# Gated expert values rounded by VectorE alone, one weight split behind them, and the next expert's row gathers put earlier

## The chip, the cores and the metric

The kernel runs on one core of one Trainium2 chip. The metric is device time: the median of three runs of the kernel before is 3069.16 us (3065.15 to 3070.6). The profile below is of one further execution of 3062.2 us.

## The reference, cut to what matters

The program is one transformer block: a projection, a chunked retention and a dilated attention, their merge, a layer norm, and then a mixture of 16 experts (4 groups of 4; each token takes 2 experts of one group), again with a layer norm behind it. All data are float32, sequence 2048, width 1024, expert width 512. The change touches only the experts:

```python
def expert_block(args):
    xblk, e = args
    hid = jax.nn.silu(xblk @ w_gate[e]) * (xblk @ w_up[e])
    return hid @ w_down[e]
```

Each token's result is weighted, added into the token's row, and the last layer norm follows.

## The kernel before

A float32 product is made of three passes of TensorE on rounded operands (type fp32r): each operand x is held as a rounded part hi and a rest lo = x - hi, and the passes are hi by hi, hi by lo, lo by hi (`passes`). Making such a pair is called a split. `split` (lines 86 to 89) lets ScalarE (ACT) write hi by a copy (line 88) and VectorE (DVE) write lo by a subtraction (line 89). In the listings a split of a weight piece is one 128x1024 row at L88 and one at L89.

The experts run one after the other, 0 to 15, in `MoE.run`; in this part of the program all engines keep the order in which the code is written. For one expert the program does this:

- `gate_up`, four times (quarters m = 0 to 3): 48 matmuls of 128x256 each (line 1288) put the gate and the up values of 256 tokens into one bank of PSUM.
- `hidden(m)`, written one quarter later than its products: ACT takes the silu of the gate half out of PSUM into a buffer s (line 1294), DVE multiplies s by the up half (line 1295), and s is split into hi and lo (lines 88 and 89).
- `part`: 36 matmuls of 128x512 (line 1315) multiply quarters 0, 1 and 2 of the hidden values by the down weights into four banks; 12 more follow for quarter 3.
- `weights(n)`: takes the next n weight pieces of 512 KB, which SP's queue has loaded into one of four raw buffers, splits each, and lets SP load the piece that is four further on into the buffer so freed (lines 1207 and 1208). An expert has 12 pieces. In quarters 0 and 1 they are the four down pieces of this expert, in quarters 2 and 3 the first two gate/up pieces of the next expert. Four more are taken in `two`, two more behind it.
- `fetch(e + 1)`: two gathers of 128 rows (line 1226, issued by POOL) bring the next expert's token rows. `turn(e + 1)` later transposes them on TensorE (line 1263) and splits them on ACT and DVE.
- `next(fin)`: one step of the last layer norm of tokens of the group of four experts before (statistics L859 and L867, two POOL operations L868 and L869, two DVE operations L1417 and L1419, and a scatter by POOL to the output, L1231). There is such work in experts 4 to 7, 8 to 11 and 12 to 15, a step in each of the first three quarters and one at the end of an expert.
- Experts with more than 256 tokens take `three` in place of `two` (in this data 3, 7, 8, 10, 11); there a branch (L1513) comes between `part` and the transposes.

POOL's DMAs (gathers, and scatters that add into `d_z`) run on the software queue q0, SP's on the hardware queue q1; both are served by the same 16 DMA engines.

Of the kernel before, what the change touches and what calls it, by code (L numbers as in the profile page):

```python
# [40 lines left out]
class Ring:  # L41
# [4 lines left out]
    def next(self):  # L46
        v = self.views[self.i % len(self.views)]
        self.i += 1
        return v
# [36 lines left out]
def split(nc, hi, lo, src, sub=None):  # L86

    nc.scalar.activation(hi, src, AF.Copy)  # L88
    (sub or nc.vector).tensor_sub(lo, src, hi)  # L89
# [1080 lines left out]
class MoE:  # L1170
# [120 lines left out]

    def hidden(self, m, ps):
        nc, s = self.g.nc, self.sr.next()
        nc.scalar.activation(s, ps[:, :256], AF.Silu)
        nc.vector.tensor_mul(s, s, ps[:, 256:])
        split(nc, *(t[:, m, :] for t in self.h), s)

    def down(self, h, idx, tag="main", sums=None, then=None, wait=True):

# [8 lines left out]
    def banks(self, blocks, tag="main"):  # L1308
        return [(b, j, self.g.bank(tag)) for b in blocks for j in range(2)]
# [170 lines left out]
    def blocks(self, e, wg, idx, fin):  # L1480

        p = []
        for m in range(4):
            p.append(self.gate_up(wg[m]))
            if m == (3 if e < NE - 1 else 2):
                self.hint(e)
            if m:
                self.hidden(m - 1, p[m - 1])
            self.weights((2, 2, 1, 1)[m])
            if m < (3 if e < NE - 1 else 1):  # L1490
                next(fin, None)
            if m == 2:
                self.fetch(e + 1)
                for b in range(2) if e % 4 == 3 else ():
                    self.gather(self.sums[b], self.g.d_z, idx[:, b, 0:1])
                if e % 4 == 3 and e < NE - 1:
                    self.list(e // 4)
                if e == NE - 2:
                    self.list(3)
        return p[3]  # L1500
# [269 lines left out]
```

## Time and profile before

| what | value |
|---|---|
| median of 3 runs | 3069.16 us |
| the profiled execution | 3062.2 us, span 3060.0 us |
| TensorE (PE) busy | 2915.3 us, 95% of the span |
| DVE, ACT, POOL busy | 1429.4, 974.4, 663.8 us |
| mean granted TensorE clock | 0.978 |
| stretch of experts 1 to 14 | 2332 to 3005 us |

A row of the timeline gives the start in us, the duration in us, the engine, the line, the operation, what it writes and reads, how many instructions are merged in it, and in brackets how long the engine sat idle before it and what ended that. A row of the waits gives the waiting engine and line, what it waited for, the sum in us, the times, and the longest. Names: `moe` are buffers of the experts (hidden values, token rows), `mw` and `m2w` are weights (raw and split), `d_x` holds the token rows, `d_z` the sums.

### The profile page before, as it was taken

The page shows a single profiled execution, that of the slowest core. Times are in us where ns is not written, and L with a number is a line of the kernel's source. Part 1 is how long each engine was busy: PE and PEld are TensorE (multiplying, and loading weights), DVE is VectorE, ACT ScalarE, POOL GpSimd, SP SyncE. Part 2 cuts the span into 40 slices and gives each one's busy share as a digit, 9 for nine tenths or more (in the row PEclk, how much of TensorE's full clock was granted, in tenths as well). Part 3 has the DMA queues.
Part 4 walks back from the last instruction along what each step waited for, and adds up shares of the span by engine and source line. Part 5 has one row for each costly group of instructions (what it writes and reads, how often), then busy time and mean ns, then how long its engine had stood idle before and what let it go on. Part 6 is the DMA issues. An engine that isn't in the chain of part 4 may idle for free. (4 is left out here: it accounts for less than half of the span.)

```text
span 3060.0 us, 44087 instructions
## 1 busy us (share of the span) xinstructions
PE 2915.3 (95%) x16140; PEld 2516.4 (82%) x16140; DVE 1429.4 (47%) x3259; ACT 974.4 (32%) x1945; POOL 663.8 (22%) x720
## 2 busy tenths in 40 slices
PE   8999999999999999999889999989998999989997
PEld 6887888888888888888668888878877988878886
DVE  3222433233335523334545665556554476444565
ACT  3221223233333322332123333323224444333342
POOL 0001311122113322100222112222432223022133
PEclk9999999999999999999899999999998999999998
DMA  6445956855766675545853444355847768365684
GB/s 208 142 181 161 199 144 161 178 142 143 160 161 164 176 162 144 143 117 175 284 204 135 155 152 141 124 176 207 146 131 204 253 216 270 124 192 168 202 275 160
DMA packets 449147, 534.14 MB, mean 175 GB/s; under 512 B 183153, under 2 KB 292849, under 8 KB 446818
## 3 DMA queue, kind: packets, MB, share of 16 engines
q1 hardware_dynamic: 261538, 417.78, 43.3%
q0 software_dynamic: 187328, 112.79, 16.1%
q8 instruction: 155, 2.54, 0.4%
q14 instruction: 126, 1.03, 0.1%
HBM read 378.12 MB, written 151.76 MB: 173 GB/s over the span
## 5 line engine op out<-in xcount | busy, mean ns | idle before, releaser
L144 PE MATMUL bank_main<-h,h 128*128 128x512 f32 x3936 | 1019.0, 403 | 10.6 <-ACT h L88 5.8
L144 PEld LDWEIGHTS bank_main<-h,h 128*128 128x128 f32 x3936 | 716.1, 190 | 149.4 <-DVE h L89 8.2
L361 ACT ACTIVATE at<-at,at 128x256 f32<-128x256 f32 (+2 forms) x384 | 174.4, 455 | 536.5 <-DVE at L359 495.9
L1288 PE MATMUL bank_main<-moe,m2w 128*128 128x256 f32 x2304 | 276.5, 281 | 7.5 <-DVE moe L1323 4.8
L1288 PEld LDWEIGHTS bank_main<-moe,m2w 128*128 128x128 f32 x2304 | 274.6, 188 | 10.2 <-issue 6.0
L359 DVE CUSTOM_DVE_ANT_0 at<-bank_att,at 128x256 f32<-128x256 f32 (+2 forms) x384 | 124.9, 362 | 214.7 <-PE bank_att L352 135.5
L1315 PE MATMUL bank_main<-mw,moe 128*128 128x512 f32 x744 | 195.9, 420 | 24.1 <-ACT moe L88 23.9
L1315 PEld LDWEIGHTS bank_main<-mw,moe 128*128 128x128 f32 x744 | 147.4, 203 | 61.9 <-ACT moe L88 27.8
L1083 PE MATMUL bank_main<-m2w,m 128*128 128x512 f32 x768 | 195.0, 407 | 1.2 <-DVE m L89 1.2
L744 PE MATMUL bank_main<-m1r,m1r 128*128 128x512 f32 x672 | 189.7, 415 | 0.0
L379 PEld LDWEIGHTS bank_att<-at,at 128*128 128x128 f32 (+1 forms) x1280 | 168.9, 192 | 13.3 <-DVE at L371 1.9
L89 DVE TENSOR_TENSOR h<-h,h 128x1024 fp32r<-128x1024 f32 x108 | 134.9, 1254 | 80.3 <-ACT h L88 79.6
L1083 PEld LDWEIGHTS bank_main<-m2w,m 128*128 128x128 f32 x768 | 144.2, 193 | 33.8 <-DVE m L89 1.9
L379 PE MATMUL bank_att<-at,at 128*128 128x64 f32 (+1 forms) x1280 | 164.4, 267 | 1.3 <-DVE at L371 1.3
L352 PE MATMUL bank_att<-at,at 128*128 128x256 f32 (+2 forms) x768 | 152.7, 326 | 3.1 <-DVE at L381 3.1
L381 DVE COPY at<-bank_att 128x128 f32<-128x128 f32 x192 | 55.4, 288 | 212.3 <-PE bank_att L379 208.8
L352 PEld LDWEIGHTS bank_att<-at,at 128*128 128x128 f32 x768 | 142.1, 233 | 13.5 <-DVE at L381 3.9
L320 POOL DMA_DIRECT2D at<-d_q x96 | 77.6, 811 | 339.6 <-PE bank_att L352 333.2
L744 PEld LDWEIGHTS bank_main<-m1r,m1r 128*128 128x128 f32 x672 | 125.2, 188 | 25.1
L319 POOL DMA_DIRECT2D at<-d_k x64 | 51.0, 814 | 417.2 <-PE bank_att L352 207.4
L89 DVE TENSOR_TENSOR m2w<-mw,m2w 128x1024 fp32r<-128x1024 f32 x78 | 95.8, 1237 | 94.0 <-ACT m2w L88 94.0
L88 ACT ACTIVATE h<-h 128x1024 fp32r<-128x1024 f32 x108 | 113.2, 1055 | 79.9 <-PE bank_main L144 45.0
(295 smaller groups left out, 4382.0 us busy)
## 6 DMA issues: line engine op xcount, KB each, us to landing
mw<-in_w_gu_dram SPq DMA_DIRECT2D x98, 512.0 KB, 6.4
h<-in_w_in_dram SPq DMA_DIRECT2D x92, 512.0 KB, 6.1
mw<-in_w_dn_dram SPq DMA_DIRECT2D x49, 512.0 KB, 5.8
at<-d_q POOLq DMA_DIRECT2D x96, 256.0 KB, 12.4
at<-d_k POOLq DMA_DIRECT2D x64, 256.0 KB, 13.8
at<-d_va SPq DMA_DIRECT2D x240, 64.0 KB, 4.2
moe<-in_w_gu_dram SPq DMA_DIRECT2D x30, 512.0 KB, 5.8
d_o<-at SPq DMA_DIRECT2D x192, 66.0 KB, 4.0
```

Of the source, the lines that this page charges most:

```text
L88: nc.scalar.activation(hi, src, AF.Copy)
L89: (sub or nc.vector).tensor_sub(lo, src, hi)
L144: self.g.nc.tensor.matmul(ps, s[:, k, c], m[:, k % 2, :], start=k + n == 0, stop=k * 3 + n == 23)
L320: done.append(nc.gpsimd.dma_start(Q[i][:, c], ap3(g.d_q, order * 1024 * T + o, [[512 * T, 2], [T, 64], [1, 512]])))
L352: nc.tensor.matmul(ps[:, e, :nk], queries(Q[e]), keys(k), start=n == 0, stop=n == 1)
L359: nc.vector.tensor_tensor_reduce(out=pe, in0=ps[:, e, :nk], in1=bv, scale=1.0, scalar=3e38, op0=OP.add, op1=OP.min, accum_out=ot[:, 128 + ...
L361: nc.scalar.activation(pe, pe, AF.Exp, scale=-1.0, bias=ot[:, 128 + e:129 + e], accum_out=ot[:, 130 + e:131 + e])
L379: nc.tensor.matmul(po[:, 64 * e:64 * e + 64], pt[:cw, e, c, :], v[:cw, c, 64 * e:64 * e + 64], start=c == 0, stop=c == nch - 1)
L744: nc.tensor.matmul(ps, a[:, kk:kk + 128], w[:, c], start=k == ks[0] and i == 0, stop=k == ks[-1] and i == 2)
L1083: nc.tensor.matmul(ps[j], a[:, kk], w[:, c], start=k + i == 0, stop=k * 3 + i == 23)
L1288: nc.tensor.matmul(ps[:, 256 * u:256 * u + 256], x[:, k, c], y[:, k, :], start=k + i == 0, stop=k * 3 + i == 23)
L1315: self.g.nc.tensor.matmul(p, a[:, k, 128 * b:128 * b + 128], w[:, 512 * j:512 * j + 512], start=k + i == 0, stop=k * 3 + i == 11)
```

## The change

`hidden` no longer uses `split`: DVE multiplies s by the up half twice, once with a rounded output (hi) and once back into s, and subtracts. In `blocks`, quarter 2 splits no weight piece and quarter 3 splits two. The gathers of the next expert's rows (and in experts 3, 7, 11 and 15 of the sums) are written in quarter 1, ahead of that quarter's layer norm step, and no longer in quarter 2 behind it.

```diff
--- before.py
+++ after.py
@@ -1291,9 +1291,11 @@
 
     def hidden(self, m, ps):
         nc, s = self.g.nc, self.sr.next()
+        hi, lo = (t[:, m, :] for t in self.h)
         nc.scalar.activation(s, ps[:, :256], AF.Silu)
+        nc.vector.tensor_mul(hi, s, ps[:, 256:])
         nc.vector.tensor_mul(s, s, ps[:, 256:])
-        split(nc, *(t[:, m, :] for t in self.h), s)
+        nc.vector.tensor_sub(lo, s, hi)
 
     def down(self, h, idx, tag="main", sums=None, then=None, wait=True):
 
@@ -1482,17 +1484,18 @@
         p = []
         for m in range(4):
             p.append(self.gate_up(wg[m]))
+            if m == 1:
+                self.fetch(e + 1)
+                for b in range(2) if e % 4 == 3 else ():
+                    self.gather(self.sums[b], self.g.d_z, idx[:, b, 0:1])
             if m == (3 if e < NE - 1 else 2):
                 self.hint(e)
             if m:
                 self.hidden(m - 1, p[m - 1])
-            self.weights((2, 2, 1, 1)[m])
+            self.weights((2, 2, 0, 2)[m])
             if m < (3 if e < NE - 1 else 1):
                 next(fin, None)
             if m == 2:
-                self.fetch(e + 1)
-                for b in range(2) if e % 4 == 3 else ():
-                    self.gather(self.sums[b], self.g.d_z, idx[:, b, 0:1])
                 if e % 4 == 3 and e < NE - 1:
                     self.list(e // 4)
                 if e == NE - 2:
```

The order on DVE in expert 10, from the hidden values of quarter 1 to the second gate/up piece (`m2w_14802`). `moe_17011` and `moe_17012` are hi and lo, `moe_17027` and `moe_17028` the two buffers s, `moe_17048` and `moe_17049` two token rows in the layer norm. Before:

```order
L1295 TENSOR_TENSOR moe_17028<-moe_17028,bank_main 128x256
L89 TENSOR_TENSOR moe_17012<-moe_17028,moe_17011 128x256
L89 TENSOR_TENSOR m2w_14802<-mw_14991,m2w_14801 128x1024
L1419 SCALAR_TENSOR_TENSOR moe_17048<-moe_17048,moe_17051,moe_17047 128x1024
L867 BN_AGGR moe_17052<-moe_17052 128x2
L1417 SCALAR_TENSOR_TENSOR moe_17049<-moe_17049,moe_17052,moe_17046 128x1024
L1295 TENSOR_TENSOR moe_17027<-moe_17027,bank_main 128x256
L89 TENSOR_TENSOR moe_17012<-moe_17027,moe_17011 128x256
L89 TENSOR_TENSOR m2w_14802<-mw_14992,m2w_14801 128x1024
```

And now:

```order
L1296 TENSOR_TENSOR moe_17011<-moe_17028,bank_main 128x256
L1297 TENSOR_TENSOR moe_17028<-moe_17028,bank_main 128x256
L1298 TENSOR_TENSOR moe_17012<-moe_17028,moe_17011 128x256
L1421 SCALAR_TENSOR_TENSOR moe_17048<-moe_17048,moe_17051,moe_17047 128x1024
L867 BN_AGGR moe_17052<-moe_17052 128x2
L1419 SCALAR_TENSOR_TENSOR moe_17049<-moe_17049,moe_17052,moe_17046 128x1024
L1296 TENSOR_TENSOR moe_17011<-moe_17027,bank_main 128x256
L1297 TENSOR_TENSOR moe_17027<-moe_17027,bank_main 128x256
L1298 TENSOR_TENSOR moe_17012<-moe_17027,moe_17011 128x256
L89 TENSOR_TENSOR m2w_14802<-mw_14991,m2w_14801 128x1024
L89 TENSOR_TENSOR m2w_14802<-mw_14992,m2w_14801 128x1024
```

The subtraction of the first gate/up piece has gone from in front of L1419 (now L1421) to behind the hidden values of quarter 2, and each multiplication is there twice.

The order on POOL in the same expert, from the scatter of a finished row on; `moe_17013` and `moe_17014` are the two buffers of the next expert's rows. Before:

```order
L1231 DMA out_dram<-moe_17057,moe_17022 2560x1024
L1504 TENSOR_LOAD const_83
L868 TENSOR_SCALAR moe_17051<-moe_17051 128x1
L869 TENSOR_TENSOR moe_17051<-moe_17051,const_80 128x1
L1231 DMA out_dram<-moe_17048,moe_17059 2560x1024
L868 TENSOR_SCALAR moe_17052<-moe_17052 128x1
L869 TENSOR_TENSOR moe_17052<-moe_17052,const_80 128x1
L1226 DMA moe_17013<-d_x_72,moe_17018 128x1024
L1226 DMA moe_17014<-d_x_72,moe_17018 128x1024
```

And now:

```order
L1231 DMA out_dram<-moe_17057,moe_17022 2560x1024
L1507 TENSOR_LOAD const_83
L1226 DMA moe_17013<-d_x_72,moe_17018 128x1024
L1226 DMA moe_17014<-d_x_72,moe_17018 128x1024
L868 TENSOR_SCALAR moe_17051<-moe_17051 128x1
L869 TENSOR_TENSOR moe_17051<-moe_17051,const_80 128x1
L1231 DMA out_dram<-moe_17048,moe_17059 2560x1024
L868 TENSOR_SCALAR moe_17052<-moe_17052 128x1
L869 TENSOR_TENSOR moe_17052<-moe_17052,const_80 128x1
```

The two gathers have moved past two pairs of L868 and L869 and one scatter to the output.

## Rows read from the trace of the kernel before

**Rows 1.** The first line of the page.

```profile
span 3060.0 us, 44087 instructions
```

**Rows 2.** Waits of PE from expert 1 to expert 14 (2332 to 3028 us), three of them.

```profile
PE bank_main L1315 <- ACT moe L88: 19.0, 8, 5.2
PE bank_att L1263 <- DMA moe<-d_x,moe: 7.8, 4, 2.7
PE bank_att L1263 <- PEq L1513: 6.2, 4, 2.5
```

**Rows 3.** Stretches of one expert each, from its first gate/up matmul to the first of the next: experts 2, 4, 5, 6, 9, 13 and 14. Columns: start and end, length, then busy time with instruction count of PE, PE's weight load, DVE, ACT and POOL, the granted clock, the share of the DMA engines' time, GB/s.

```profile
2368.00:2403.40 35.40, 35.40 (x257) 33.41 (x256) 19.79 (x24) 19.48 (x29) 6.52 (x6) 1.00 0.85 274
2460.20:2495.80 35.60, 35.56 (x256) 33.56 (x257) 27.83 (x36) 14.74 (x23) 7.80 (x8) 1.00 0.64 224
2495.80:2538.20 42.40, 38.88 (x258) 35.39 (x257) 27.53 (x34) 19.66 (x29) 16.25 (x14) 0.92 0.81 262
2538.20:2577.80 39.60, 36.16 (x257) 33.19 (x256) 27.34 (x34) 19.44 (x29) 13.51 (x12) 1.00 0.80 254
2714.20:2757.90 43.70, 38.51 (x256) 35.15 (x257) 27.33 (x34) 20.05 (x30) 18.32 (x15) 0.92 0.84 262
2923.50:2964.30 40.80, 37.67 (x258) 34.35 (x257) 27.24 (x34) 19.64 (x29) 15.48 (x14) 0.96 0.83 267
2964.30:3004.90 40.60, 37.28 (x257) 34.54 (x256) 27.53 (x34) 19.59 (x29) 13.50 (x12) 0.96 0.77 253
```

**Rows 4.** PE's timeline at L1315, in experts 4, 5, 9, 10 (two rows), 11 and 13.

```profile
2483.04 8.42 PE L1315 MATMUL bank_main<-mw,moe 128*128 128x512 f32 x36
...
2520.73 7.16 PE L1315 MATMUL bank_main<-mw,moe 128*128 128x512 f32 x30 [0.66 <-ACT moe L88]
...
2744.05 9.54 PE L1315 MATMUL bank_main<-mw,moe 128*128 128x512 f32 x30 [4.66 <-ACT moe L88]
...
2780.65 1.54 PE L1315 MATMUL bank_main<-mw,moe 128*128 128x512 f32 x6
2785.34 8.73 PE L1315 MATMUL bank_main<-mw,moe 128*128 128x512 f32 x30 [3.15 <-ACT moe L88]
...
2852.53 9.88 PE L1315 MATMUL bank_main<-mw,moe 128*128 128x512 f32 x30 [5.22 <-ACT moe L88]
...
2950.81 8.62 PE L1315 MATMUL bank_main<-mw,moe 128*128 128x512 f32 x30 [3.03 <-ACT moe L88]
```

**Rows 5.** Timeline of expert 10 on ACT and DVE, from the copy of its last down piece to the hidden values of quarter 2.

```profile
2773.94 1.06 ACT L88 ACTIVATE mw<-moe 128x1024 fp32r<-128x1024 f32 x1 [2.83 <-DMA moe<-in_w_dn_dram]
...
2775.03 1.23 DVE L89 TENSOR_TENSOR mw<-moe,mw 128x1024 fp32r<-128x1024 f32 x1 [2.67 <-ACT mw L88]
...
2778.81 0.41 DVE L1295 TENSOR_TENSOR moe<-moe,bank_main 128x256 f32<-128x256 f32 x1
2779.25 0.42 ACT L88 ACTIVATE moe<-moe 128x256 fp32r<-128x256 f32 x1 [3.98 <-DVE moe L1295]
...
2780.65 1.22 DVE L89 TENSOR_TENSOR m2w<-mw,m2w 128x1024 fp32r<-128x1024 f32 x1 [0.52 <-ACT m2w L88]
...
2781.79 1.28 DVE L1419 SCALAR_TENSOR_TENSOR moe<-moe,moe,moe 128x1024 f32<-128x1024 f32 x1
...
2783.22 1.28 DVE L1417 SCALAR_TENSOR_TENSOR moe<-moe,moe,moe 128x1024 f32<-128x1024 f32 x1
...
2784.43 0.41 DVE L1295 TENSOR_TENSOR moe<-moe,bank_main 128x256 f32<-128x256 f32 x1
2784.87 0.42 ACT L88 ACTIVATE moe<-moe 128x256 fp32r<-128x256 f32 x1 [3.99 <-DVE moe L1295]
```

**Rows 6.** The same in expert 11: the multiplication of quarter 1, the copy of the first gate/up piece, the silu of quarter 2.

```profile
2845.42 0.41 DVE L1295 TENSOR_TENSOR moe<-moe,bank_main 128x256 f32<-128x256 f32 x1
...
2849.38 1.06 ACT L88 ACTIVATE m2w<-mw 128x1024 fp32r<-128x1024 f32 x1 [3.10 <-DMA mw<-in_w_gu_dram]
2850.34 0.36 ACT L1294 ACTIVATE moe<-bank_main 128x256 f32<-128x256 f32 x1
```

**Rows 7.** POOL's timeline in expert 10: the last scatter ahead of the layer norm step, its first operation, and the two gathers.

```profile
2763.70 1.72 POOL L1231 DMA_INDIRECT out_dram<-moe,moe  x1 [1.14 <-DVE moe L1419]
2776.47 1.32 POOL L868 TENSOR_SCALAR moe<-moe 128x1 f32<-128x1 f32 x1 [11.04 <-DVE moe L867]
...
2786.68 1.75 POOL L1226 DMA_INDIRECT moe<-d_x,moe  x1 [0.19 <-issue]
2788.73 0.95 POOL L1226 DMA_INDIRECT moe<-d_x,moe  x1 [0.30 <-issue]
```

**Rows 8.** DMA in five stretches. Rows of issues: what is loaded, queue, count, KB, us to landing; the three are issued at 2762.3 (expert 10's last down piece), near 2781.9 (expert 10) and at 2835.4 (expert 11). Rows of queues: packets, MB, share of the 16 engines' time; the first two from 2764 to 2772 us, the third from 2772 to 2775 us.

```profile
moe<-in_w_dn_dram SPq DMA_DIRECT2D x1, 512.0 KB, 11.7
...
q0 software_dynamic: 365, 1.33, 62.4%
q1 hardware_dynamic: 531, 0.99, 38.4%
...
q1 hardware_dynamic: 579, 1.15, 99.6%
...
mw<-in_w_gu_dram SPq DMA_DIRECT2D x1, 512.0 KB, 3.8
...
mw<-in_w_gu_dram SPq DMA_DIRECT2D x1, 512.0 KB, 14.0
```

## The prediction

> **What bounds the kernel now.** I read the page first for the span [rows 1], then PE's waits over the experts, then the experts one by one as windows, and last the timeline of the engines where PE waits. PE is busy 95% of the span, so time can only go where PE stands still or runs at a lower clock. From expert 1 to 14 two waits belong to the edited code [rows 2]: the down products (L1315) wait 19.0 us in 8 places for the ACT copy that writes hi of the hidden values, and the transposes of the next rows (L1263) wait 7.8 us in 4 places for the gather. The windows show the whole price [rows 3]: experts 2 and 4 take 35.4 and 35.6 us with PE never idle, while 5, 6, 9, 13 and 14, with the same products, take 42.4, 39.6, 43.7, 40.8 and 40.6. Their sum is 207.1; five times 35.6 is 178.0; so 29.1 us are lost there, more than the waits alone, since after a wait the granted clock is lower (0.92 in 5 and 9) and matmuls last longer. Experts 10 and 11 go through the branch, so I take them from the matmuls: 30 of them last 7.16 us after a short wait, 8.73 after 3.15 us and 9.88 after 5.22 us [rows 4]. That is 3.15 + 1.57 = 4.7 us and 5.22 + 2.72 = 7.9 us. In both, the lost time is 1.5 times the wait; I use that factor below. In all 29.1 + 4.7 + 7.9 = 41.7 us are within reach. The third wait of [rows 2], 6.2 us at the branch, is one of PE's own sequencer, and I leave it as it is.
>
> Why hi is late is seen in expert 10 [rows 5]. The last down piece lands late and ACT copies it at 2773.94; DVE subtracts at 2775.03, runs its layer norm step, and multiplies quarter 1 at 2778.81. Then come ACT's hi, the rest lo, the subtraction of a gate/up piece (from 2780.65), L1419, L1417, the multiplication of quarter 2 at 2784.43, ACT's hi at 2784.87, and PE at 2785.34. So DVE's order is the limit, with a trip to ACT inside it. In expert 11 it is ACT's order [rows 6]: the silu of quarter 2 stands behind the copy of a gate/up piece that waited 3.10 us for its DMA.
>
> **The change part by part.** *Second multiplication for ACT's copy.* DVE gets one more 0.41 us instruction for each quarter, ACT loses one of 0.42. Before, from the start of the multiplication to the end of lo were 0.41, a hand-over, 0.42, a hand-over and a subtraction of about the same length, 1.3 us; now three DVE instructions make about 1.25. So DVE's chain is no longer, and hi exists 0.45 us earlier.
>
> *Weight split moved.* Its subtraction, with the wait in front of it, took DVE from about 2780.1 to 2781.79, 1.7 us, ahead of quarter 2's values; now it is behind them. The new chain in expert 10: 2778.81 + 1.25 = 2780.06; L1419 takes 1.2 from start to start; from there to the next multiplication are 2784.43 - 2782.99 = 1.44; 2780.06 + 1.2 + 1.44 = 2782.7; the rounded product ends at 2783.1. Before, hi ended at 2785.3: 2.2 us earlier. PE stood ready at 2785.34 - 3.15 = 2782.19, so it waits 0.9 us. With the same 2.2 us, expert 13 goes from 3.03 to 0.8 [rows 4], expert 9 from 5.2 to 3.0, and the waits in 5, 6 and 14 go. (The four long ones make 16.1 of the 19.0 us; of the other 2.9 some 0.5 is a stop in 9 just ahead of its long one, 2.4 are left for 5, 6 and 14.) In expert 11 ACT's silu no longer stands behind the DMA wait: quarter 1's chain starts at 2845.42, quarter 2's follows at about 2846.7 and PE needs it at 2852.53 - 5.22 = 2847.3; nothing is left of that wait. What stays is (3.0 + 0.9 + 0.8) x 1.5 = 7 us.
>
> What the moved split may cost: the piece's raw buffer comes free later, behind quarter 2's lo, so SP loads the piece that is the third of `two` later, and ACT's copies of the turned rows are queued behind that piece's copy; PE's next gate/up products wait for those. The cover is the 36 down products of 8.42 us [rows 4]. By the near row, a load issued at that point of an expert lands in 3.8 us [rows 8]: 1.5 + 1.2 + 3.8 and two copies of 1.06 end about 8.6 us after the down products start, while the turned rows can first be copied near 9.1. Cost nothing to a few tenths; I take 1.5 us in all. The far row is 14.0 us to landing (expert 11, where gathers and scatters ran beside it); that end is a rival.
>
> *Gathers moved.* POOL now issues them behind the scatter of 2763.70 and ahead of L868 at 2776.47, where it sat idle 11.04 us, against 2786.68 and 2788.73 [rows 7]: 20 us earlier. They cost POOL 2.7 us of that idle time. The 7.8 us of waits in 5, 6 and 14 go (their clock loss is in the windows). In experts 3, 7 and 11 POOL had nothing in front of the gathers, so they hardly move. The cost is on the DMA engines: the gathers, 1 MB, now queue on q0 behind the scatters while q1 still has weights to bring. From 2764 to 2772 both queues ran and q1 moved 0.99 MB in 8 us (0.12 MB/us); from 2772 it was alone and moved 1.15 MB in 3 us (0.38) [rows 8]. The last down piece, issued at 2762.3 and landing 11.7 us later, is what DVE's chain begins with. Had it still to come wholly at 0.12 rather than 0.38 MB/us, it would land 0.52/0.12 - 0.52/0.38 = 2.9 us later; but its copy starts at 2773.94, only 2 us after q0 ran empty, and the 0.99 MB are nearly all of the two down pieces in flight. Bounds 0 and 2.9; I take a third of a us in the three experts that still wait, 1 x 1.5 = 1.5 us. On the gain side the later pieces find the engines freer; I leave it at nothing, up to 2 us.
>
> The Trainium skill, page "DMA: Bandwidth & Descriptors", section "Queues, rings and completion order", says that each DMA engine takes turns between the queue rows for which it has work, a packet at a time. The two rates agree with that; by it alone, gathers put beside weight loads always halve them, and the sum would be the first rival's. The trace has both: q0 was nearly drained when the piece landed.
>
> **Sum.** 41.7 - 7 - 1.5 - 1.5 = 31.7 us. The profiled execution of 3062.2 us becomes 3030.5; it stood 7.0 below the median, and I carry the difference over to the median: 3069.2 - 31.7 = 3037.5, said as 3037.
>
> **The rivals.** *Gathers slow the last down piece (chance 0.15).* At 2.9 us the chain is later than the 2.2 us won: 9, 10 and 13 keep their waits of 5.2 + 3.15 + 3.03 = 11.4 us and a little more, about 12 x 1.5 = 18 us instead of 7, and 5, 6, 14 keep 2.4 x 1.5 = 3.6. The gather waits and expert 11 are still won: 41.7 - 18 - 3.6 - 1.5 = 18.6, so 3050.6. For it speaks q1's rate beside q0; against it the order of arrival above.
>
> *The DMA engines bound the experts (0.08).* Their share is 0.81 to 0.84 of 42.4 to 43.7 us [rows 3], that is 34 to 37 us of work for a 35.6 us expert. If 0.86, just over the 0.85 of expert 2, is the most that can be had, 5, 6, 9, 13 and 14 stop at 39.9, 36.8, 42.7, 39.4 and 36.4: 17.2 us remain of the 29.1, the gain is 41.7 - 17.2 - 1.4 = 23, and the time 3046. Against it: the share stood near 1 (62.4 + 38.4%) for 8 us on end, so 0.86 is no ceiling.
>
> *The late pieces in `two` (0.12, of which 0.05 slower).* One mechanism: the two gate/up pieces that are loaded after quarter 2's values land so late that ACT copies them when PE wants the turned rows. In 5, 6, 9, 13 and 14 each us past the 8.6 above costs 1.5. It eats the whole 31.7 when the landing takes 3.8 + 31.7/(5 x 1.5) = 8.0 us; there is the 0.07 for no change. At 10 us it is 6.2 x 7.5 = 46 us: 3069.2 + 14.8 = 3084, slower. For it the 14.0 us of expert 11, against it that the gathers that ran there are just what leaves this place.
>
> **How the numbers follow.** The forecast has 0.65, the others 0.15, 0.08, 0.07 and 0.05. Faster by over 0.2% (6 us, about what a measurement of this kernel tells from no change): the first three, 0.88; same 0.07; slower 0.05. The forecast's own range is 3026 (nothing left of 41.7, the freer engines won) to 3044 (both DMA terms tripled). The range, 3025 to 3055, takes in the first two rivals with some us of margin and leaves out the late pieces.
>
> **What would show it.** Waits of PE at the down products for DVE now, about 5 us in three experts (9 most) instead of 19.0; no wait of L1263 for the gather; experts 5, 6 and 14 near 36 us, 13 near 37, 9 near 40; the gathers issued within 4 us of the scatter; DVE's L1298 directly behind two multiplications. Wrong would be: the last down piece copied over 2 us later against the start of its expert; L1288 or the copies of the turned rows waiting for a gate/up piece's landing; windows that stay above 39 us with a DMA share near 0.9.

## The result and the profile after

| | before | after |
|---|---|---|
| median of 6 runs each | 3067.15 us (3060.76 to 3076.35) | 3047.47 us (3043.08 to 3051.78) |
| ratio | | 0.9933, interval 0.9917 to 0.9949 |
| profiled execution | 3062.2 us | 3043.1 us |

The gain is 20.5 us by the ratio (19.1 between the two profiled executions) where 31.7 were forecast. Lines of the code stand two or three further down than before: the silu is L1295, the three DVE instructions of the hidden values are L1296 to L1298, the down products L1317, ACT's copies of their sums L1333, the branch L1516.

The first line of the page and PE's waits from expert 1 to 14, which answer to [rows 1, 2]. Columns: waiting line, releaser, us in all, times, longest.

```profile
span 3041.1 us, 44162 instructions
...
PE bank_att L1263 <- PEq L1516: 9.2, 4, 3.3
...
PE bank_main L1317 <- DVE moe L1297: 3.9, 2, 2.5
PE bank_main L1317 <- DVE moe L1296: 3.3, 3, 2.5
PE bank_main L1288 <- ACT moe L1333: 2.9, 3, 1.4
PE bank_att L1263 <- issue: 1.8, 1, 1.8
...
PE bank_main L1317 <- DVE moe L1298: 0.5, 3, 0.2
```

The waits for gathered rows are gone (7.8 before), and those for the hidden values fell from 19.0 us to 7.7 (3.9 + 3.3 + 0.5). But one wait grew, that at the branch: 9.2 us where 6.2 stood.

Stretches of experts 2, 5, 6, 9, 13 and 14, as in [rows 3].

```profile
2369.60:2405.50 35.90, 35.78 (x258) 33.51 (x258) 22.67 (x30) 19.02 (x26) 7.74 (x6) 1.00 0.86 280
2500.60:2539.20 38.60, 36.26 (x257) 33.21 (x257) 28.88 (x38) 18.37 (x25) 15.69 (x14) 1.00 0.89 284
2539.20:2574.70 35.50, 35.50 (x258) 33.44 (x257) 28.92 (x38) 18.37 (x25) 14.36 (x12) 1.00 0.89 282
2709.20:2751.20 42.00, 38.90 (x257) 34.96 (x258) 28.82 (x38) 18.99 (x26) 18.41 (x15) 0.92 0.86 272
2913.10:2949.00 35.90, 35.70 (x257) 33.25 (x256) 27.69 (x37) 17.14 (x24) 14.65 (x13) 1.00 0.91 290
2949.00:2985.00 36.00, 35.83 (x256) 33.61 (x257) 29.62 (x40) 18.61 (x26) 15.29 (x12) 1.00 0.91 284
```

6, 13 and 14 are now as fast as an undisturbed expert, at full granted clock and with the DMA engines busy for 0.89 to 0.91 of the time; 5 and 9 are not.

Expert 10, which answers to [rows 5, 7]: POOL's last scatter and the two gathers, ACT's copy of the last down piece, DVE from quarter 1's values to quarter 2's, and PE.

```profile
2757.23 1.39 POOL L1231 DMA_INDIRECT out_dram<-moe,moe  x1 [0.30 <-issue]
2758.93 0.97 POOL L1226 DMA_INDIRECT moe<-d_x,moe  x1 [0.30 <-issue]
2760.20 0.95 POOL L1226 DMA_INDIRECT moe<-d_x,moe  x1 [0.30 <-issue]
...
2766.22 1.06 ACT L88 ACTIVATE mw<-moe 128x1024 fp32r<-128x1024 f32 x1 [2.52 <-DMA moe<-in_w_dn_dram]
...
2771.09 0.41 DVE L1296 TENSOR_TENSOR moe<-moe,bank_main 128x256 fp32r<-128x256 f32 x1
2771.53 0.42 DVE L1297 TENSOR_TENSOR moe<-moe,bank_main 128x256 f32<-128x256 f32 x1
2771.99 0.42 DVE L1298 TENSOR_TENSOR moe<-moe,moe 128x256 fp32r<-128x256 f32 x1
2772.33 1.28 DVE L1421 SCALAR_TENSOR_TENSOR moe<-moe,moe,moe 128x1024 f32<-128x1024 f32 x1
...
2774.96 0.41 DVE L1296 TENSOR_TENSOR moe<-moe,bank_main 128x256 fp32r<-128x256 f32 x1
...
2776.34 6.70 PE L1317 MATMUL bank_main<-mw,moe 128*128 128x512 f32 x28 [0.18 <-DVE moe L1298]
```

The gathers go out right behind the scatter, and the last down piece is copied 15.1 us after the expert's first matmul (2751.16); before it was 16.0 (2773.94 against 2757.94). No split stands between the two quarters: from multiplication to multiplication are 3.9 us, before 5.6.

Expert 11, which answers to [rows 6]: ACT's copies of two gate/up pieces and the silu of quarter 3, DVE's subtraction for the second piece and its two products, PE's fourth bank of down products, and the first transposition behind the branch.

```profile
2838.52 1.06 ACT L88 ACTIVATE m2w<-mw 128x1024 fp32r<-128x1024 f32 x1 [5.14 <-DMA mw<-in_w_gu_dram]
2840.91 1.06 ACT L88 ACTIVATE m2w<-mw 128x1024 fp32r<-128x1024 f32 x1 [1.32 <-DMA mw<-in_w_gu_dram]
2841.87 0.36 ACT L1295 ACTIVATE moe<-bank_main 128x256 f32<-128x256 f32 x1
...
2842.00 1.23 DVE L89 TENSOR_TENSOR m2w<-mw,m2w 128x1024 fp32r<-128x1024 f32 x1 [1.16 <-ACT m2w L88]
2843.14 0.41 DVE L1296 TENSOR_TENSOR moe<-moe,bank_main 128x256 fp32r<-128x256 f32 x1
2843.59 0.42 DVE L1297 TENSOR_TENSOR moe<-moe,bank_main 128x256 f32<-128x256 f32 x1
...
2844.16 3.71 PE L1317 MATMUL bank_main<-mw,moe 128*128 128x512 f32 x9 [2.49 <-DVE moe L1297]
...
2851.14 1.57 PE L1263 MATMUL bank_att<-const,moe 128*128 128x128 f32 x8 [3.28 <-PEq L1516]
```

Quarter 2's values are in time here. But both gate/up pieces now stand ahead of the silu of quarter 3 and wait for their DMA, and DVE subtracts the second piece before it multiplies (2843.14). The fourth bank of down products is the one that held quarter 3's gate and up values; it is free only when DVE has read them (L1297), and PE waits 2.49 us. Then it waits 3.28 us at the branch. Expert 11 takes 65.1 us, as before.

By expert, from first gate/up matmul to the next one's: 5, 6, 9, 13 and 14 won 3.8, 4.2, 1.8, 4.9 and 4.6 us, expert 10 won 3.5, expert 8 1.8, expert 11 nothing; expert 3 lost 2.8, expert 1 lost 1.6, the last one 1.0, expert 2 0.4. That makes the 18.9 us by which the span fell.

### The profile page after: what moved, and what is told of

Read it like the earlier page. It is cut to its first block, busy times and chain, and to the rows that moved or that the text cites. A ratio compares the mean times of both kernels' runs of the same rounds, so it can differ in the third digit from the quotient of the medians.

```text
span 3041.1 us, 44162 instructions
## 1 busy us (share of the span) xinstructions
PE 2911.8 (96%) x16140; PEld 2512.8 (83%) x16140; DVE 1453.0 (48%) x3319; ACT 952.6 (31%) x1885; POOL 666.9 (22%) x720
## 5 line engine op out<-in xcount | busy, mean ns | idle before, releaser
L1317 PE MATMUL bank_main<-mw,moe 128*128 128x512 f32 x744 | 189.6, 410 | 13.4 <-DVE moe L1296 8.6
L1317 PEld LDWEIGHTS bank_main<-mw,moe 128*128 128x128 f32 x744 | 142.5, 197 | 48.2 <-DVE moe L1296 10.6
L352 PEld LDWEIGHTS bank_att<-at,at 128*128 128x128 f32 x768 | 142.1, 233 | 13.4 <-DVE at L381 3.8
L88 ACT ACTIVATE h<-h 128x1024 fp32r<-128x1024 f32 x108 | 113.2, 1055 | 76.8 <-PE bank_main L144 44.9
```

What stands on the lines that cost most here:

```text
L352: nc.tensor.matmul(ps[:, e, :nk], queries(Q[e]), keys(k), start=n == 0, stop=n == 1)
L1317: self.g.nc.tensor.matmul(p, a[:, k, 128 * b:128 * b + 128], w[:, 512 * j:512 * j + 512], start=k + i == 0, stop=k * 3 + i == 11)
```

## The experiments

Letters: **D** is the DVE edit of the hidden values, **S** the moved split, **G** the earlier gathers; the changed kernel is DSG. Times stand as ratios to the kernel before of the same chip, with 5 to 12 runs each; 0.001 is 3.1 us.

**Gate/up splits behind quarter 3's values.** One split goes behind `hidden(3)`; for both it is (2, 2, 0, 0) and `weights(2)`:

```diff
-            self.weights((2, 2, 0, 2)[m])
+            self.weights((2, 2, 0, 1)[m])
...
                 self.hidden(3, p3)
+                self.weights(1)
```

> The changed kernel, with one of quarter 3's two splits moved behind the hidden values of quarter 3. Theory (the hidden values of quarter 3 wait in ACT's and DVE's order behind two gate/up pieces that have not landed, and the fourth bank of down products waits for them): in expert 11 the copy of silu no longer follows the second piece, so PE's wait before the fourth bank falls from 2.5 us to 0.5 to 1.2 us, in expert 1 from 1.4 to about 0.3 us; over all the kernel is 2 to 6 us faster than the changed one, about 3043 against 3047. Rival (the branch waits of PE's sequencer, 12 us in all, or the earlier gathers ate what was forecast): expert 11 stays at 65 us and the time within 1 us of the changed kernel's.

> The changed kernel, with both splits of quarter 3 moved behind the hidden values of quarter 3. Theory: no gate/up piece stands ahead of silu of quarter 3, so PE's wait before the fourth bank goes in experts 1, 9 and 11 (2.5 us in expert 11 to under 0.3); expert 11 takes 58 to 61 us instead of 65.1, expert 1 35.5 instead of 37.1; the time is 4 to 9 us below the changed kernel's, about 3040. Against it: the pieces are split some 1 to 2 us later and their next loads are issued later, which would show as new waits of the products for a split in the next experts, and would eat up to 4 us. Rival (branch waits or gathers): expert 11 stays at 65 us.

Measured: 0.9933 (0.9919 to 0.9947) with one, 0.9927 (0.9910 to 0.9944) with both; neither can be told from the changed kernel, while 2 to 6 and 4 to 9 us less than its time were expected. (The branch waits are 9.2 us, not the 12 of the first text.) With one, expert 1 is back at 35.5 us (as it is in a second profile of the changed kernel, so this says nothing of the move), and the fourth bank's wait in expert 11 is gone but for 0.2 us, yet the expert takes 63.5 us, because the transposes then wait 4.8 (the profile names the gather from d_z; the last section has another reading). With both it takes 58.8, within what was expected. The kernel with both, PE in expert 11 and a row of its waits over experts 1 to 14:

```profile
2837.41 8.41 PE L1317 MATMUL bank_main<-mw,moe 128*128 128x512 f32 x36
2848.42 1.06 PE L1263 MATMUL bank_att<-const,moe 128*128 128x128 f32 x8 [2.61 <-PEq L1516]
...
PE bank_main L1288 <- ACT moe L1333: 6.5, 8, 1.4
```

The down products run through without a stop. The price is in the last row: ACT's copies of the sums stand later in its order, and the next expert's gate/up products wait 6.5 us for them instead of 2.9; experts 2, 6 and 14 are 1.1, 1.8 and 1.5 us longer than in the changed kernel. So the reading of the fourth bank is right, but the missing gain does not come back with it in the measured times. In the single profiled executions experts 1 to 14 take 646.5 us with one and 642.1 with both, in the two of the changed kernel 652.5 and 650.0. The part of the program ahead of them, which no edit touches, took from 2332 to 2342 us in the fourteen profiled executions, and that hides a few us.

**One part undone.** In the first the splits are handed out as before, (2, 2, 1, 1): DG. In the second the gathers are back behind quarter 2's products: DS.

```diff
-            self.weights((2, 2, 0, 2)[m])
+            self.weights((2, 2, 1, 1)[m])
```

```diff
-            if m == 1:
-                self.fetch(e + 1)
-                for b in range(2) if e % 4 == 3 else ():
-                    self.gather(self.sums[b], self.g.d_z, idx[:, b, 0:1])
...
             if m == 2:
+                self.fetch(e + 1)
+                for b in range(2) if e % 4 == 3 else ():
+                    self.gather(self.sums[b], self.g.d_z, idx[:, b, 0:1])
```

> The changed kernel with the splits handed out as before (two, two, one, one), so that one split stands again between the hidden values of quarters 1 and 2 and of quarter 3. By the sum of the prediction the moved split is worth the larger part of the gain: the waits before the down products in experts 9, 10, 11 and 13 come back but for the 0.45 us of the earlier high half; expert 11's 5 us wait returns at quarter 2. Time then 3054 to 3060. Theory of the result (the move gives back in expert 11 and expert 1 what it takes elsewhere): expert 1 is back at 35.5, expert 11 about 65, experts 9, 10 and 13 together 4 to 7 us longer than in the changed kernel; time 3050 to 3056. Rival (the move is worth nothing): within 1 us of the changed kernel.

> The changed kernel with the gathers of the next expert back behind quarter 2's products. Theory: only the transposes' wait for the gathered rows returns, 7.8 us over the experts in the kernel before, 1.4 to 1.5 times that with the clock, less what hidden values are late anyway: 6 to 11 us slower than the changed kernel, 3053 to 3058, spread over experts 5, 6, 13 and 14; expert 11 stays at 65 us. Rival (earlier gathers take the queues from the weight pieces and so make expert 11's piece late): expert 11's gate/up piece lands earlier and expert 11 falls to about 60 us, and the time is within 3 us of the changed kernel's.

Measured: DG 0.9956 (0.9940 to 0.9972), so beside the other two the move is worth 7 us by the changed kernel's 0.9933 and 1 us by its second measurement, 0.9952 (below): a gain is not shown. Expert 11 takes 64.4 us with 4.5 of wait at quarter 2, as the theory had it, but 9, 10 and 13 together are 1.6 us longer, not 4 to 7. DS 1.0038 (1.0023 to 1.0052): 11.6 us slower than the kernel before, where 3053 to 3058 us, faster than before, were expected. Neither theory nor rival held. DS's waits, experts 1 to 14:

```profile
PE bank_att L1263 <- DMA moe<-d_x,moe: 21.6, 9, 3.8
PE bank_att L1263 <- PEq L1515: 14.2, 4, 6.3
PE bank_main L1317 <- DVE moe L1296: 5.2, 6, 2.5
```

The hidden values are early, and the time is spent at the next two stations: the gathered rows (21.6 us, before 7.8) and the branch (14.2, before 6.2). That made the other cells of the table necessary.

**Parts alone and in pairs.** Each is the kernel before with hunks of the change and no other. D has the first hunk (`hidden`), G the gathers at m == 1, and S one line; GS has both of these. The changed kernel and GS are run a second time, side by side.

```diff
-            self.weights((2, 2, 1, 1)[m])
+            self.weights((2, 2, 0, 2)[m])
```

> The kernel before, with the edit of the hidden values alone (high half by DVE, no copy on ACT). With the moved split but not the gathers the kernel was 11.6 us slower than before. Theory (the transposes wait for whichever is later, down products or gathered rows; the rows are gathered behind the norm's instructions on POOL, of which one takes 1.40 us instead of 0.57 beside the new DVE order): the gathers are issued up to 1.2 us later than before, so the transposes' waits for rows rise from 7.8 us to 11 to 18 us and eat the 0.45 us a quarter that the hidden values gain; time 0 to 8 us slower than before. Rival (the lateness comes from the moved split alone): POOL's instruction stays at 0.57 us, and the time is 2 to 6 us faster than before.

> The kernel before, with the gathers moved ahead alone. Theory: the 7.8 us of waits for gathered rows go, in experts 5, 6 and 14, with 1.3 to 1.5 times that in time; the waits for the hidden values (23.9 us) stay whole. Time 8 to 12 us faster than before. Rival (the gain belongs to the pair of edits): under 4 us faster.

> The changed kernel without the edit of the hidden values: gathers ahead and one split moved, the hidden values rounded by ACT's copy as before. By the factors measured so far the moved split is worth about 7 us beside the gathers, and the DVE edit the rest. Theory of the prediction (both shorten one chain, 1.65 us by the split and 0.45 us by the DVE edit): 14 to 18 us faster than before, 3 to 6 us slower than the changed kernel. Rival (the two are the same saving and one of them is enough): within 1.5 us of the changed kernel.

> The kernel before, with the moved split alone; it completes the table of the three edits, of which seven are measured. Theory (the three share one loop of gathers, norms, splits and weight loads, and neither of the other two is worth anything while the gathers lie behind quarter 2's products: DVE alone +10.7 us, DVE and split +11.6 us): between 4 us faster and 4 us slower than before; the waits for the hidden values fall below 15 us, those for gathered rows rise above 7.8. Rival (the moved split is worth its 1.65 us a quarter by itself, as the prediction's sum had it): 7 to 14 us faster.

> The changed kernel again, beside the two kernels below on one chip. From 18 to 23 us faster than before, as it was.

> Gathers ahead and moved split without the DVE edit, again, beside the changed kernel. If the DVE edit is worth nothing here (theory after eight runs): within 4 us of the changed kernel, on either side. If it is worth the 0.45 us a quarter of the prediction: 3 to 6 us slower than the changed kernel.

Measured, with PE's waits over experts 1 to 14 (for hidden values: L1315 or L1317 on ACT's L88 or DVE's L1295 to L1298; for rows: L1263 on the gather from d_x; at the branch: L1263 on PE's sequencer) and, in the last column, the time of these experts in the same profiled execution:

| kernel | ratio (interval) | hidden | rows | branch | sum, us | experts 1 to 14, us |
|---|---|---|---|---|---|---|
| before | 1 | 19.0 | 7.8 | 6.2 | 33.0 | 672.4 |
| S | 1.0003 (0.9990 to 1.0016) | 7.0 | 16.0 | 12.8 | 35.8 | 675.0 |
| D | 1.0035 (1.0020 to 1.0049) | 16.6 | 14.2 | 5.8 | 36.6 | 681.8 |
| DS | 1.0038 (1.0023 to 1.0052) | 7.9 | 21.6 | 14.2 | 43.7 | 686.4 |
| G | 0.9968 (0.9954 to 0.9982) | 19.6 | 0 | 6.7 | 26.3 | 658.8 |
| DG | 0.9956 (0.9940 to 0.9972) | 14.7 | 0 | 5.2 | 19.9 | 651.7 |
| GS | 0.9924 (0.9908 to 0.9941) | 8.0 | 0 | 11.2 | 19.2 | 657.1 |
| GS again | 0.9950 (0.9932 to 0.9969) | 7.8 | 0 | 10.7 | 18.5 | 652.9 |
| DSG, changed | 0.9933 (0.9917 to 0.9949) | 7.7 | 0 | 9.2 | 16.9 | 652.5 |
| DSG again | 0.9952 (0.9932 to 0.9972) | 6.1 | 0 | 10.9 | 17.0 | 650.0 |

(In GS again 4.7 of the 10.7 us are a wait of expert 11 that its profile puts down to the gather from d_z, at the same instruction. Waits of L1263 for nothing that the profile names are left out: 3.2 us in D, 1.1 in DG, 1.8 and 1.5 in the changed kernel. So are the waits of the gate/up products for ACT's copies of the sums: 6.7 and 5.9 us in GS, 2.7 to 3.0 in the others.)

The text for G gives 23.9 us as the waits for hidden values in the kernel before; they are 19.0. The rows of S, of D and of G that stand behind the table:

```profile
PE bank_att L1263 <- DMA moe<-d_x,moe: 16.0, 9, 2.9
PE bank_att L1263 <- PEq L1513: 12.8, 4, 4.5
PE bank_main L1315 <- ACT moe L88: 5.8, 3, 2.4
```

```profile
PE bank_main L1317 <- DVE moe L1296: 15.2, 7, 4.2
PE bank_att L1263 <- DMA moe<-d_x,moe: 14.2, 7, 3.0
```

```profile
PE bank_main L1315 <- ACT moe L88: 19.6, 8, 4.7
```

What follows. S takes some 12 us from the waits for hidden values, alone or beside G, and alone it gives all of it back: rows +8.2, branch +6.6. Its time, that of G (9.8 us) and D's waits for rows came as the theory had them; D's time, 10.7 us, lies past the 8 that were the most expected, and the changed kernel's second run, 14.7 us faster, below its 18 to 23. S beside G brings 13.5 us where both ran on one chip, and 5.5 by the second GS, on another. D beside G and S brings nothing that the time shows: GS and the changed kernel are within 2.8 us of each other in the first comparison, with GS the faster, and within 0.6 in the second. Each of these differences is uncertain by some 7 us, so the upper end of the 3 to 6 us that the sum gave D is not there, while 3 us are not excluded. The last column, of single executions, does not separate them either: beside G it is 651.7 us with D, 657.1 and 652.9 with S, 652.5 and 650.0 with both, where two executions of one kernel differ by 4.2 and 2.5. So the rival "one of the two is enough" fits and is not proved.

D's 0.45 us itself is there where a wait shows it. The long wait of the down products in expert 9, first in GS, then in the changed kernel:

```profile
2744.08 9.12 PE L1315 MATMUL bank_main<-mw,moe 128*128 128x512 f32 x30 [2.91 <-ACT moe L88]
```

```profile
2737.22 9.60 PE L1317 MATMUL bank_main<-mw,moe 128*128 128x512 f32 x30 [2.46 <-DVE moe L1296]
```

The second profile of each has 2.92 and 2.46.

D alone costs 10.7 us. Expert 6 on POOL, first in D, then in the kernel before:

```profile
2573.82 1.40 POOL L869 TENSOR_TENSOR moe<-moe,const 128x1 f32<-128x1 f32 x1
2575.41 1.06 POOL L1226 DMA_INDIRECT moe<-d_x,moe  x1 [0.19 <-POOLq L1596]
```

```profile
2564.10 0.57 POOL L869 TENSOR_TENSOR moe<-moe,const 128x1 f32<-128x1 f32 x1
2564.86 1.76 POOL L1226 DMA_INDIRECT moe<-d_x,moe  x1 [0.19 <-issue]
```

With the expert's start at 2546.45 and 2538.19, the gather is issued at 29.0 us instead of 26.7. 0.83 us of it is the small operation in front: in D, DS and the changed kernel one of an expert's two takes 1.39 to 1.53 us in most of the experts with a norm, while in the kernel before and in S all take 0.57 or 0.58. The rest is the norm's step on DVE, which comes later; the last down piece is copied 16.0 us into the expert instead of 13.9. Why the piece is later with D was not tried. With G the gathers no longer stand behind this operation, which fits that D costs nothing there.

**The mark of the branch.** The changed kernel, with the mark that names the branch to PE set behind quarter 1's products:

```diff
-            if m == (3 if e < NE - 1 else 2):
+            if m == (1 if e < NE - 1 else 2):
                 self.hint(e)
```

> The changed kernel, with the mark that tells PE of the branch set after quarter 1's products instead of quarter 3's. Theory (PE stands at the branch until code that an instruction queue moves has landed; in expert 11 this queue waits behind 15 us of full DMA engines; PE's first instruction behind the branch came 3.1 to 3.3 us after the queue's packet wherever it waited over 2.5 us): the packets move some 11 us earlier, the four waits fall from 9.2 us to 2.5 (0.6 each), expert 11 from 65.1 to about 61, expert 10 from 61.3 to 58.5, expert 3 from 59.6 to 58; time 5 to 9 us below the changed kernel. Rival (the mark does not set when the code is fetched, or it is fetched and lost again): the waits stay between 6 and 15 us and the time within 2 us of the changed kernel.

Measured: 0.9920 (0.9905 to 0.9935), not to be told from the changed kernel, with branch waits of 9.3 us (4.6 in expert 11); another 4.9 us of the transposes, in experts 5 and 13, have no name in its profile. The rival holds: the place of the mark does not set these waits.

**GS with one split behind quarter 3's values.** The edit of the first experiment on GS:

> As the last, and one of quarter 3's two splits moved behind the hidden values of quarter 3. Expert 1 is back at 35.5 us (37.2 without), the wait before the fourth bank in expert 11 falls from 1.3 us to under 0.5. If that is all, 2 to 5 us faster than the kernel without it; if the copies of the down products by ACT come late behind the split in exchange (4.7 us against 2.9 in the kernel with one split behind), within 2 us of it.

Measured: 0.9934 (0.9915 to 0.9953). Expert 1 is at 35.5 us (as it is in GS again, without the move) and expert 11 at 62.1 without any wait for the fourth bank, while the gate/up products wait 7.4 us for ACT's copies (6.7 and 5.9 in GS). None of the versions with G and S can be told from the changed kernel; a kernel that beats it was not found.

## Why the prediction was right in sign and too large

**Right.** The gathers: no wait for rows is left, the last down piece was not delayed in expert 10, and G alone is worth 9.8 us (1.5 times the 7.8 us of waits are 11.7). The waits that were to stay: 3.1 us in expert 9 where 3.0 were forecast, 0.2 in expert 10 (0.9), none in 13 (0.8). In expert 10 the last of it is luck: the two edits won the 2.2 us that were forecast (1.7 between the multiplications and 0.45 by the earlier hi), and the other 0.9 went because the last down piece happened to come 0.9 us earlier. How much hangs on that piece is seen with G alone: the split still stands between the quarters, the piece is copied 13.4 us into the expert instead of 16.0, and the wait is 0.8 us instead of 3.15. Experts 6, 10, 13 and 14 came out at 35.5, 61.3, 35.9 and 36.0 us. The time lies in the range, and outside the likeliest case's own 3026 to 3044.

**The step that failed: "nothing is left of that wait" in expert 11, together with "the third wait ... I leave it as it is".** Of the 12.8 us between 31.7 and the span's 18.9, expert 11 makes 7.9. Quarter 2's wait did go; but the step did not ask what is late next. Two things were. The first is the silu of quarter 3 behind two pieces that have not landed; the prediction priced the moved split only by the later loads in `two`, not by what it puts in front of quarter 3. The second is the branch. In eleven executions of nine kernels the first transposition of expert 11 came 37.2 to 41.1 us after its start, although the down products ahead of it ended anywhere from 32.7 to 39.6; only the three kernels with a split behind quarter 3's values came below, at 36.6, 35.6 and 33.8. In the kernel before, the 5.2 us for the hidden values covered most of this wait, and 0.6 showed.

**Terms that were mis-sized.** In 5, 6, 9, 13 and 14 the forecast was 29.1 - 5.7 = 23.4 us, and 19.2 came. Expert 5 is 3.0 short: PE stood 1.8 us ahead of the transposes for nothing that the profile names, and 0.6 us for hidden values, because the last down piece is copied 15.4 us into the expert where it was 13.5 (quarter 1's multiplication follows that copy by 4.9 us in both kernels). The 1.8 us are probably the branch again: `two` stands behind the same `if` as `three` (last section). Expert 9 is 1.8 short: its 3.1 us of waits cost 6.4 over an undisturbed expert, a factor of 2.1 and not 1.5, with the granted clock at 0.92 as before. The other experts lost 4.0 us net where 3.0 had been set aside. Part of this is the execution: in a second profile of the same kernel expert 1 is at 35.5 us, expert 3 at 57.7 and expert 11 at 68.0. That profile's branch waits, and the first transposition of its expert 11:

```profile
PE bank_att L1263 <- PEq L1516: 10.9, 4, 6.0
...
2855.28 1.94 PE L1263 MATMUL bank_att<-const,moe 128*128 128x128 f32 x8 [6.02 <-PEq L1516]
```

**What the sum's form hid.** It added what each edit takes away. The table shows that the waits follow one another on PE, in each expert first for hidden values and then for rows or at the branch, so that an edit is worth only what lies above the next of them. And an edit can make the next one later, as D does with the gathers: the hidden part alone (DS) is not 20 us of gain (31.7 less 1.5 times 7.8) but 11.6 of loss. The 0.45 us of earlier hi in each quarter are seen in one wait of expert 9 and not in the time.

**Rivals.** Gathers that slow the last down piece: not seen by more than 0.4 us in the three experts for which it was priced. The piece is copied 0.9 us earlier in expert 10, 1.6 earlier in 13 and 0.4 later in 9; of 5, 6 and 14 only 5 has it clearly later, by 1.9 us, and there it is as late with D alone (15.5 us), whose gathers go out late. The Trainium skill, page "DMA: Bandwidth & Descriptors", section "Queues, rings and completion order", says that each DMA engine takes turns between the queue rows for which it has work; by that alone the piece should have come later wherever the gathers went out earlier, and the trace of 10 and 13 does not show it. That the time is close to this rival's 3050.6 has other causes. The DMA engines as the bound: 6, 13 and 14 run at shares of 0.89 to 0.91 without loss, so 0.86 was no ceiling. Late pieces in `two`: not seen in 6, 13 and 14.

## What to carry to other kernels

When a wait is to be removed, look at the same place for the next thing to arrive (rows, code, a bank that must come free) and count only the distance to it. Parts of a change that work on one chain do not add up: of these three, S alone gains nothing and D alone loses, and the gain appears when the last arrival, the gathered rows, is moved first. A split moved out of one quarter's way stands in the next one's, so ask what it waits for there.

## What was not expected of the hardware

**Code for the branch.** Beside q0 and q1 the trace has two queues named instruction. In expert 11 of the changed kernel, first the queues from 2833 to 2847 us, then from 2847.5 to 2848.5 (packets, MB, share of the engines' time):

```profile
q0 software_dynamic: 969, 3.52, 62.5%
q1 hardware_dynamic: 959, 2.21, 40.5%
...
q1 hardware_dynamic: 98, 0.36, 92.2%
q8 instruction: 1, 0.02, 6.8%
q0 software_dynamic: 10, 0.01, 3.4%
q14 instruction: 1, 0.01, 2.1%
```

For 14 us both queues together filled the engines; then a single packet of q8 came (2848.0, to a quarter of a us), and 3.1 us later PE's first instruction behind the branch. In ten of fourteen executions this distance in expert 11 is 3.0 to 3.3 us, with the packet anywhere from 30.7 to 36.4 us after the expert's start; in the other four it is 3.6 to 4.6. Counted from the end of the packet, which takes 1.0 to 2.5 us there, it is 1.9 to 2.2 us in thirteen of the fourteen; the other is the kernel before, where the hidden values came last. In expert 10 it is 2.0 to 2.3 us in all fourteen. Three of the thirteen are waits that the profile puts down to the gather from d_z, so these are probably the same wait. So are probably the six waits of the transposes without a name (1.1 to 3.2 us, in experts 5, 9 and 13): in all six a packet of q8 ends 1.6 us ahead. The Trainium skill, page "Runtime: NRT & Kernel Launch", section "Instruction fetch mechanics", says that an engine's instructions are fetched in blocks of 16 KiB by a DMA queue, and that a taken branch whose target is not at hand must wait for such a fetch. The single packet of 0.02 MB ahead of each of these waits agrees. That the packet is PE's is argued from these distances. That it is late because the engines are full is not shown: in the kernel with both splits behind quarter 3's values it came at 30.7 us with the engines just as full, and moving the mark did not move it (34.8 us against 35.6 and 36.9). What sets its time stays open.

**A small POOL operation that depends on DVE's order.** L869, 128x1, takes 0.57 us or 1.40. In D's expert 6 it starts 0.25 us behind the start of DVE's subtraction for a weight piece (2573.57 to 2574.79) and ends 0.4 us after that one's end. In the kernel with both splits behind quarter 3's values, which has the same three DVE instructions for the hidden values, no call takes over 0.63 us. That the two hinder each other fits this and was not tried by itself.
